# Attention's softmax join and division: from VectorE to GpSimd

## The chip, the cores and the metric

The kernel runs on one core of one Trainium2 chip. The metric is the device time of one execution, in microseconds (us); lower is better. The engines are named as in the profile: PE is TensorE's matmuls and PEld its weight loads, DVE is VectorE, ACT is ScalarE, POOL is GpSimd, SP is SyncE, which issues most of the transfers.

## The reference

One layer of a decoder on 1024 tokens of width 1024 in float32. A normalised input is projected; two token mixers work on the projections; their outputs are gated, merged, projected and added to the input; a gated MLP with a short convolution follows, and a last normalisation. The change is in the two mixers:

```
# differential attention, 4 heads, causal, two softmaxes a head
logits = where(dist >= 0, s - slope * dist, NEG_INF)
p = softmax(logits)
a = p[:, :, 0] - lam * p[:, :, 1]
o = a @ v
o = rmsnorm(o, subln_w) * (1.0 - lam_init)

# sliding-window attention, 8 heads, window 128, one sink logit a head
p = softmax(concatenate([logits, sink], axis=-1))[..., :-1]
o = p @ v
```

## The kernel before

Matmuls run with operands split into a rounded high part and a low part (`wh`, `wl`; `xh`, `xl`), three matmuls for one product. The attention runs as six units in a row: the four heads of the differential attention (`da_step`, `da_av`, `da_norm`), and the two groups of four heads of the windowed attention (`sw_step`). Each unit goes over eight blocks of 128 queries.

A step of the differential attention, `da_step(h, i)`, has width w = (i + 1) * 128, from 128 to 1024 columns. For each of the two softmaxes, c = 0 and 1, TensorE makes the scores into a PSUM tile `sc` (L619); DVE adds the bias, writes the tile `L` and keeps the row's minimum (L623, with a read of its accumulator); ScalarE takes the exponential in place with the row's sum (L624). The first softmax is not divided by its sum: the head's normalisation, `da_norm`, takes that out. So only one factor, -lam * sum0 / sum1, is needed, made by a reciprocal (L627) and a small product (L628), and the join is one DVE instruction (L629). TensorE then turns the joined tile in blocks of 128 x 128 (L635), ScalarE copies the turned blocks out of PSUM as the high part `aT` (L637), DVE subtracts for the low part (L638), and after every second step `da_av` multiplies with the values (L647 to L649).

The L tiles have four buffers (`bufs=4`), so two steps fit in; the aT tiles have five. GpSimd clears the unused half of an aT tile (L602) and takes the power in the head's normalisation (L170).

A step of the windowed attention, `sw_step(g, n)`, holds four heads of up to 256 keys in one L tile: scores (L707), the sink's column copied in by GpSimd (L711), four reductions by DVE (L714), four exponentials (L716), one reciprocal for four sums (L717), a column cleared by GpSimd (L719), four divisions by DVE (L721), transpositions (L728), copies (L731, L732), the product with the values (L738) and the output (L740, L745).

Between these, TensorE works on the projections of the gates, which nothing in the attention needs (`back_half`, matmuls of the tile `g` at L153 to L155). How many halves of them go to each step is written in the table `HALVES`; the scheduler of the framework sets the final order of each engine's instructions by its own estimates, and fixes it when the program is built. Each engine then runs its list in order.

`self.last`, set at the last division, holds back one later product of GpSimd (L776, in `rest`) by an explicit dependency.

Of the kernel before, what the change touches and what calls it, by code (L numbers as in the profile page):

```python
# [13 lines left out]
ALU = mybir.AluOpType  # L14
# [28 lines left out]
class Trunk:  # L43
# [561 lines left out]
    def da_step(self, h, i, st, aT):  # L605
        nc, ap = self.nc, self.ap
        q, k = st
        slope = 4.0 ** -(h + 1)
        w = (i + 1) * P

        lo = P if w == 640 else 0
        cuts = ((0, 256),) if i == 0 else ((0, w),) if w <= H2 else ((0, H2 - lo), (H2 - lo, w))
        pr = []
        for c in range(2):
            sc = self.tl(self.psS, [P, T], "sc")
            qs = q[c][:, i * P:(i + 1) * P]
            for part in range(2):
                for n0, n1 in cuts:
                    nc.tensor.matmul(sc[:, lo + n0:lo + n1], qs, k[c][part][:, n0:n1], start=part == 0, stop=part == 1)  # L619
            L = self.tl(ap, [P, T], "L", bufs=4)  # L620
            s = self.tl(self.st, [P, 4], "sm", bufs=8)
            o = 896 - i * P
            nc.vector.tensor_tensor_reduce(L[:, :w], sc[:, lo:lo + w], self.bias[:, o:o + w], slope, 3e38, ALU.add, ALU.min, s[:, 0:1])  # L623
            nc.scalar.activation(L[:, :w], L[:, :w], AF.Exp, bias=s[:, 0:1], scale=-1.0, accum_out=s[:, 1:2] if c else self.s0[:, i:i + 1])  # L624
            pr.append(L)

        nc.vector.reciprocal(s[:, 2:3], s[:, 1:2])  # L627
        nc.vector.tensor_scalar(s[:, 3:4], self.s0[:, i:i + 1], s[:, 2:3], self.neglam, ALU.mult, ALU.mult)  # L628
        nc.vector.scalar_tensor_tensor(pr[0][:, :w], pr[1][:, :w], s[:, 3:4], pr[0][:, :w], ALU.mult, ALU.add)  # L629
        qo = (i % 2) * P  # L630
        for j0 in range(0, i + 1, 4):
            nj = min(4, i + 1 - j0)
            ps = self.tl(self.psT, [P, 4, P], "t")
            for j in range(nj):
                nc.tensor.transpose(ps[:, j, :], pr[0][:, (j0 + j) * P:(j0 + j + 1) * P], self.ident)  # L635
            hi, lo = aT[j0 // 4, 0], aT[j0 // 4, 1]
            nc.scalar.copy(hi[:, :nj, qo:qo + P], ps[:, :nj, :])  # L637
            nc.vector.tensor_tensor(lo[:, :nj, qo:qo + P], ps[:, :nj, :], hi[:, :nj, qo:qo + P].bitcast(F32), ALU.subtract)  # L638
# [57 lines left out]
    def sw_step(self, g, n, st):  # L696
        nc, ap = self.nc, self.ap
        q, k = st
        k0 = max(n - 1, 0) * P
        w = P if n == 0 else 256  # L700
        bo = T + (P if n == 0 else 0)
        sc = self.tl(self.psS, [P, 4, 256], "sc")
        s = self.tl(self.st, [P, 4, 4], "sw", bufs=4)
        L = self.tl(ap, [P, 4, 256], "L", bufs=4)
        for h in range(4):
            for part in range(2):
                nc.tensor.matmul(sc[:, h, :], q[h][:, n * P:(n + 1) * P], k[part][:, k0:k0 + 256], start=part == 0, stop=part == 1)  # L707


        a, at, we = (0, w, w + 1) if n == 0 else (1, 0, w)  # L710
        nc.gpsimd.tensor_copy(L[:, :, at:at + 1], self.nsink[:, 4 * g:4 * g + 4].unsqueeze(2))  # L711
        for h in range(4):
            slope, ns = 2.0 ** -(4 * g + h + 1), self.nsink[:, 4 * g + h:4 * g + h + 1]
            nc.vector.tensor_tensor_reduce(L[:, h, a:w], sc[:, h, a:w], self.bias[:, bo + a:bo + w], slope, ns, ALU.add, ALU.min, s[:, 0, h:h + 1])  # L714
        for h in range(4):
            nc.scalar.activation(L[:, h, :we], L[:, h, :we], AF.Exp, bias=s[:, 0, h:h + 1], scale=-1.0, accum_out=s[:, 2, h:h + 1])  # L716
        nc.vector.reciprocal(s[:, 3, :], s[:, 2, :])  # L717
        if n:
            nc.gpsimd.memset(L[:, :, 0:1], 0.0)  # L719
        for h in range(4):  # L720
            self.last = nc.vector.tensor_scalar(L[:, h, a:w], L[:, h, a:w], s[:, 3, h:h + 1], None, ALU.mult)  # L721
        po = self.tl(self.psT, [P, H2], "t")
        nblk = w // P
        parts = []
        for b in range(nblk):
            ps = self.tl(self.psT, [P, 4, P], "t")
            for h in range(4):
                nc.tensor.transpose(ps[:, h, :], L[:, h, b * P:(b + 1) * P], self.ident)  # L728
            pt = self.tl(ap, [P, 2, 4, P], "aT", F32R, bufs=5)
            hi, lo = pt[:, 0], pt[:, 1]  # L730
            nc.scalar.copy(hi, ps)  # L731
            nc.vector.tensor_tensor(lo, ps, hi.bitcast(F32), ALU.subtract)  # L732
            parts.append((hi, lo))
        for b, (hi, lo) in enumerate(parts):
            kb = k0 // P + b
            va = self.vsw[kb // 4][:, kb % 4, g]
            for m, pt in enumerate((hi, lo)):
                nc.tensor.matmul(po, va, pt, start=b == 0 and m == 0, stop=b == nblk - 1 and m == 1)  # L738
        t = self.tl(self.gpool, [P, 4, P], "g", bufs=2)[0:64]
        nc.scalar.copy(t, po[64:128].rearrange("p (h q) -> p h q", h=4))  # L740
        pv = po[0:64].rearrange("p (c e q) -> p c e q", c=2, e=2)
        tv = t.rearrange("p (c e) q -> p c e q", e=2)
        y = self.tl(ap, [P, 2, P], "ys", bufs=3)
        for e in range(2):
            nc.vector.tensor_tensor(y[64 * e:64 * e + 64], pv[:, :, e], tv[:, :, e], ALU.add)  # L745
        self.store(self.yd[4 + 2 * g:6 + 2 * g, :, n * P:(n + 1) * P].rearrange("c p q -> p c q"), y)
# [525 lines left out]
```

## Time and profile before

| what | before |
|---|---|
| median of 3 runs | 1345.26 us (1344.66 to 1346.1) |
| span of the profiled execution, first to last instruction | 1343.0 us |
| mean granted TensorE clock | 0.997 |
| differential attention, about | 258 to 398 us |
| windowed attention, about | 398 to 485 us |

The profile shows one execution: its span is 1343.0 us, and a run's time is some 2.3 us above that, as the time includes what lies around the first and the last instruction. Only the span is known of the profiled execution itself. In rows of groups stand the line, the engine, the operation, the tile written and the tiles read, the shape, the count, then the busy time in us, the mean of one in ns, and the idle time just before them with what ended it. A busy TensorE is not a TensorE at its peak: the ends of matmuls are modelled, and a matmul's length overlaps the next one's.

### The profile page before, as it was taken

To read this page: it belongs to the slowest core of one execution; us is meant where nothing else is said; L and a number is where in the kernel's file an instruction comes from. 1 tells how busy PE (TensorE), PEld (TensorE's weight loads), DVE (VectorE), ACT (ScalarE), POOL (GpSimd) and SP (SyncE) were. 2 spreads that over 40 slices of the span, in tenths; PEclk is the share of its full clock that TensorE was granted. 3 is DMA by queue.
4 is the path that set the end of the run, shared out by engine and by line. 5 is a ranking of instruction groups with operands and counts; after the bars stand their busy time and mean duration, and the time that the engine had idled before them with its cause. 6 is when DMAs were issued, how large, how long until landed. Compare 5 with 4: busy or idle time off the path is not lost.

```text
span 1343.0 us, 17167 instructions
## 1 busy us (share of the span) xinstructions
PE 1326.8 (99%) x6304; PEld 1105.7 (82%) x6304; DVE 1052.5 (78%) x1425; ACT 602.3 (45%) x929; POOL 488.8 (36%) x364
## 2 busy tenths in 40 slices
PE   8999999999999999999999999999999999999997
PEld 6888888888888878888888888888888888788886
DVE  7846775388898976445669999999999998967454
ACT  8432232276667774344444434343434345432433
POOL 0346652000101016642446566666666611131011
PEclk9999999999999999999999999999999999999998
DMA  7244443966554245324522222222222239642342
GB/s 258 108 146 162 148 149 119 273 170 189 143 148 144 70 155 206 141 95 130 167 79 95 79 79 85 88 79 79 88 85 80 86 128 320 220 145 98 94 141 79
DMA packets 63812, 179.49 MB, mean 134 GB/s; under 512 B 7024, under 2 KB 16880, under 8 KB 63728
## 3 DMA queue, kind: packets, MB, share of 16 engines
q1 hardware_dynamic: 52272, 161.22, 36.8%
q10 hardware_dynamic: 11456, 17.18, 3.5%
q8 instruction: 50, 0.82, 0.2%
q14 instruction: 34, 0.28, 0.1%
HBM read 129.61 MB, written 48.76 MB: 133 GB/s over the span
## 4 chain that ended last, share of the span: by engine, by line
PE 72%; DVE 15%; issue 8%; DMA 2%; ACT 1%; POOL 1%; SPq 0%; POOLq 0%; DVEq 0%; ACTq 0%
PE t L887 24%; PE g L153 4%; PE g L154 4%; PE g L155 4%; DVE c L1031 3%; PE y L1056 3%; PE d L1056 3%; PE sc L154 3%; PE sc L155 3%; PE sc L153 3%; PE d L887 3%; PE sc L619 3%; PE y L887 2%; DVE wl L113 2%; DMA hr<-hd 2%
## 5 line engine op out<-in xcount | busy, mean ns | idle before, releaser
L1020 POOL TENSOR_TENSOR us<-us,rstd 128x1024 f32<-128x1024 f32 x42 | 92.6, 2225 | 85.0 <-DVE us L452 47.6
L1029 ACT ACTIVATE c<-us,vecs 128x1024 f32<-128x1024 f32 x44 | 54.8, 1248 | 118.3 <-POOL us L1020 113.8
L132 ACT CAST wh<-raw 128x1024 fp32r<-128x1024 f32 (+2 forms) x58 | 58.7, 1012 | 107.9 <-PE sc L154 35.8
L134 DVE TENSOR_TENSOR wl<-raw,wh 128x1024 fp32r<-128x1024 f32 (+2 forms) x58 | 78.3, 1352 | 32.5 <-ACT wh L132 22.8
L113 DVE TENSOR_TENSOR sl<-sf,sh 128x1024 fp32r<-128x1024 f32 x62 | 89.3, 1442 | 12.8 <-ACT sh L111 12.8
L111 ACT CAST sh<-sf 128x1024 fp32r<-128x1024 f32 x62 | 64.5, 1042 | 61.6 <-PE t L887 44.0
L97 POOL TENSOR_TENSOR sf<-rv 128x512 f32<-128x512 f32 x30 | 51.3, 1711 | 93.6 <-DVE sl L113 51.1
L1031 DVE SCALAR_TENSOR_TENSOR c<-us,vecs,c 128x1024 f32<-128x1024 f32 x44 | 75.4, 1746 | 2.7 <-ACT c L1029 2.7
L99 POOL TENSOR_TENSOR sf<-raw,rv 128x512 f32<-128x512 f32 x30 | 56.7, 1891 | 46.3 <-DVE sl L113 46.3
L1032 DVE SCALAR_TENSOR_TENSOR c<-us,vecs,c 128x1024 f32<-128x1024 f32 x44 | 73.2, 1696 | 0.0
L153 PE MATMUL g<-xh,wh 128*128 128x512 f32 x176 | 71.0, 403 | 1.5 <-ACT g L548 1.5
L154 PE MATMUL g<-xl,wh 128*128 128x512 f32 x176 | 70.3, 400 | 0.0
L155 PE MATMUL g<-xh,wl 128*128 128x512 f32 x176 | 70.3, 399 | 0.0
L170 POOL TENSOR_TENSOR rs<-ms,mhalf 128x8 f32<-128x8 f32 (+2 forms) x9 | 13.5, 1499 | 155.5 <-DVE ms L168 149.4
L1012 ACT ACTIVATE c<-c 128x1024 f32<-128x1024 f32 x22 | 23.4, 1064 | 89.6 <-DVE c L1032 89.6
L113 DVE TENSOR_TENSOR wl<-raw,wh 128x1024 fp32r<-128x1024 f32 (+1 forms) x35 | 61.8, 1765 | 0.3 <-ACT wh L111 0.2
L602 POOL MEMSET aT<- 128x128 f32 x32 | 6.1, 204 | 151.5 <-PE t L648 101.2
L623 DVE CUSTOM_DVE_ANT_0 L<-sc,bias 128x128 f32<-128x128 f32 (+7 forms) x64 | 47.8, 752 | 16.6 <-PE sc L619 13.7
L98 POOL TENSOR_TENSOR sf<-sf,raw 128x512 f32<-128x512 f32 x31 | 58.2, 1877 | 2.2
L624 ACT ACTIVATE L<-L,sm 128x128 f32<-128x128 f32 (+7 forms) x64 | 49.6, 778 | 20.0 <-DVE sm L623 17.3
L776 POOL TENSOR_TENSOR gr<-gr,rstd 128x1024 f32<-128x1024 f32 x16 | 40.3, 2523 | 43.9 <-DMA gr<-gd 43.7
L113 DVE TENSOR_TENSOR wl<-rv,wh 128x512 fp32r<-128x512 f32 x30 | 54.0, 1800 | 2.6 <-ACT wh L111 2.6
(435 smaller groups left out, 4338.4 us busy)
## 6 DMA issues: line engine op xcount, KB each, us to landing
u<-qd SPq DMA_DIRECT2D x72, 256.0 KB, 6.4
raw<-in_w_down SPq DMA_DIRECT2D x27, 512.0 KB, 3.7
hr<-hd SPq DMA_DIRECT2D x50, 256.0 KB, 4.8
raw<-in_w_up SPq DMA_DIRECT2D x23, 512.0 KB, 3.5
raw<-in_w_in SPq DMA_DIRECT2D x22, 512.0 KB, 3.8
hd<-c SPq DMA_DIRECT2D x22, 512.0 KB, 2.6
rv<-in_w_up SPq DMA_DIRECT2D x21, 512.0 KB, 3.5
gr<-gd SPq DMA_DIRECT2D x16, 512.0 KB, 3.4
```

The costliest lines, as they stand in the source:

```text
L111: cast = nc.scalar.copy(hi, src)
L113: low = nc.vector.tensor_tensor(lo, src, hi.bitcast(F32), ALU.subtract)
L132: self.hi = nc.scalar.copy(wh, raw)
L134: self.lo = (eng or nc.vector).tensor_tensor(wl, raw, wh.bitcast(F32), ALU.subtract)
L153: nc.tensor.matmul(ps, wh[:, kc + o, :], ah, start=first and n == 0, stop=False)
L154: nc.tensor.matmul(ps, wh[:, kc + o, :], al, start=False, stop=False)
L155: nc.tensor.matmul(ps, wl[:, kc + o, :], ah, start=False, stop=last and n == len(kcs) - 1)
L887: nc.tensor.matmul(ps, (ah, ah, al)[p][:, k, :], (bh, bl, bh)[p], start=first and n == p == 0, stop=last and p == 2 and n == len(ks) - 1, ...
L1020: i = (nc.vector if m % NF == 0 else nc.gpsimd).tensor_tensor(us[:, 2:], us[:, 2:], self.rstd, ALU.mult)
L1031: nc.vector.scalar_tensor_tensor(c, us[:, 1:T + 1], cw[1], c, ALU.mult, ALU.add)
L1032: nc.vector.scalar_tensor_tensor(c, us[:, 0:T], cw[0], c, ALU.mult, ALU.add)
L1056: nc.tensor.matmul(ps, v[:, n, :], x, start=n == i == 0, stop=n == len(js) - 1 and i == 2)
```

## The change

The join of the two softmaxes, one instruction of DVE, becomes two instructions of GpSimd: a product by a scalar per row, in place in the second tile, and an addition into the first. The four divisions of a windowed step go to GpSimd as they are. Lines behind the first edit move down by one.

```diff
         nc.vector.reciprocal(s[:, 2:3], s[:, 1:2])
         nc.vector.tensor_scalar(s[:, 3:4], self.s0[:, i:i + 1], s[:, 2:3], self.neglam, ALU.mult, ALU.mult)
-        nc.vector.scalar_tensor_tensor(pr[0][:, :w], pr[1][:, :w], s[:, 3:4], pr[0][:, :w], ALU.mult, ALU.add)
+        nc.gpsimd.tensor_scalar(pr[1][:, :w], pr[1][:, :w], s[:, 3:4], None, ALU.mult)
+        nc.gpsimd.tensor_tensor(pr[0][:, :w], pr[0][:, :w], pr[1][:, :w], ALU.add)
...
         for h in range(4):
-            self.last = nc.vector.tensor_scalar(L[:, h, a:w], L[:, h, a:w], s[:, 3, h:h + 1], None, ALU.mult)
+            self.last = nc.gpsimd.tensor_scalar(L[:, h, a:w], L[:, h, a:w], s[:, 3, h:h + 1], None, ALU.mult)
```

The framework's scheduler builds a new order from this: in the attention, the instructions of all engines stand in another order than before.

## The prediction

> **What bounds the kernel now.** I read the page first, then a table of the two attention stages by time, then TensorE's matmuls in the second of them.
>
> ```profile
> span 1343.0 us, 17167 instructions
> PE 1326.8 (99%) x6304; PEld 1105.7 (82%) x6304; DVE 1052.5 (78%) x1425; ACT 602.3 (45%) x929; POOL 488.8 (36%) x364
> ```
> ```profile
> 258.00:398.00 140.00, 139.92 (x877) 122.15 (x877) 118.53 (x310) 93.55 (x220) 11.50 (x37) 1.00 0.63 167
> 398.00:458.00 60.00, 59.57 (x367) 51.24 (x366) 54.75 (x191) 45.95 (x131) 5.87 (x22) 1.00 0.38 118
> 458.00:485.00 27.00, 25.40 (x137) 20.30 (x136) 25.07 (x81) 19.49 (x55) 1.67 (x7) 1.00 0.28 86
> ```
>
> Behind the length of each stretch stand the busy times of PE, weight loads, DVE, ACT and POOL, then clock and DMA. TensorE is busy nearly all the time, and the changed lines run only here: differential attention from 258 to 398 us, the windowed attention from 398 to 485. DVE is busy for 85% of the first and 92% of the second ((54.75 + 25.07) of 87), GpSimd for 8 to 9%. So DVE is a near second bound, and GpSimd is idle.
>
> A busy share hides short waits, so I price the matmuls. From the chain of waits, and from the groups of TensorE between 398 and 485 us:
>
> ```profile
> 248.56 0.87 PE t L589 x8
> 1247.69 5.44 PE y L1056 x24
> ```
> ```profile
> L153 PE MATMUL g<-xh,wh 128*128 128x512 f32 x54 | 22.5, 416 | 1.5 <-ACT g L548 1.5
> L154 PE MATMUL g<-xl,wh 128*128 128x512 f32 x54 | 22.0, 408 | 0.0
> L155 PE MATMUL g<-xh,wl 128*128 128x512 f32 x53 | 21.5, 406 | 0.0
> L728 PE MATMUL t<-ident,L 128*128 128x128 f32 x116 | 19.1, 275 | 0.2 <-DVE ys L745 0.2
> L738 PE MATMUL t<-aT,v 128*128 128x512 f32 x56 | 18.7, 404 | 0.4 <-DVE aT L732 0.4
> L707 PE MATMUL sc<-u,u 128*128 128x256 f32 x112 | 18.5, 291 | 0.0
> ```
>
> A matmul of 512 columns advances TensorE by 5.44 / 24 = 0.227 us, one of 256 by half of that, a transposition by 0.87 / 8 = 0.109. The rows make 217 x 0.227 + 112 x 0.113 + 116 x 0.109 = 74.6 us; the other 59 of the 504 matmuls are small and make at most 6.7. So about 81 of 87 us are work, and nearly 6 us are waits and change-overs. The first stretch, counted in the same way, has about 6 of 140. That is the ceiling of any gain: TensorE's work is not changed. As change-overs stay, I put the waits at 2.5 us in the first stage and at 4 us in the second.
>
> **What is removed and added.** DVE's groups in the attention stages, then GpSimd's instructions by line (shortest, median and longest ns):
>
> ```profile
> L629 DVE SCALAR_TENSOR_TENSOR L<-L,sm,L 128x128 f32<-128x128 f32 (+7 forms) x32 | 26.1, 816 | 0.6
> L721 DVE TENSOR_SCALAR L<-L,sw 128x255 f32<-128x255 f32 (+1 forms) x64 | 18.5, 341 | 0.4
> ```
> ```profile
> L776 POOL TENSOR_TENSOR gr<-gr,rstd x16: 2392/2406/3406, 488.1 to 582.3; 128x1024 f32<-128x1024 f32 x16
> L848 POOL TENSOR_TENSOR rstd<-rstd,t x14: 1288/1662/1843, 614.5 to 683.3; 128x512 f32<-128x512 f32 x14
> L602 POOL MEMSET aT<- x32: 204/204/207, 236.4 to 391.5; 128x128 f32 x32
> L1019 POOL MEMSET us<- x44: 89/99/122, 684.8 to 1097.3; 128x2 f32 x44
> ```
>
> DVE loses 26 us of 118 and 18 of 80, some 67 to 78% stay busy. GpSimd gets 32 multiplications, 32 additions and 64 divisions. The addition has two inputs: the first two rows give 0.17 us plus (2.406 - 1.288) / 512 = 2.18 ns a column. The multiplication and the division read one tensor and a scalar per row; before has no such row on GpSimd. From below I bound it by the memsets, which only write: 0.10 us plus (204 - 99) / 126 = 0.83 ns a column. From above stands the two-input rate. I take the memset rate, as a stream with one input is nearer to it, and keep the other end for the range. At width 1024 the multiplication is then 0.95 us (dear: 2.41) and the addition 2.41, at 896 0.84 and 2.12, at 768 0.74 and 1.84, one division of 255 columns 0.31 (dear: 0.73). For a head's eight widths (4608 columns) that makes 16 us of GpSimd in some 34: throughput is enough. What counts is the length of each step's chain: at the mean width of 576 a step has 0.58 + 1.42 = 2.0 us on GpSimd where DVE had 0.82, at 1024 it has 3.4.
>
> The Trainium skill ("GPSIMD Engine Reference", section 4.1) says the same of one-input operations, about line rate, but advises against two-input arithmetic there, as about half as fast as on VectorE. No run so far shows the first. By its figure of one element a cycle at 1.2 GHz, 1024 columns would be an estimated 0.85 us, and the sum would fall by about half a microsecond.
>
> **The first stage.** The chain of a step, from groups by form of 258 to 398 us:
>
> ```profile
> L623 DVE CUSTOM_DVE_ANT_0 L<-sc,bias 128x1024 f32<-128x1024 f32 x8 | 9.7, 1216 | 0.1
> L628 DVE TENSOR_SCALAR sm<-s,sm,neglam 128x1 f32<-128x1 f32 x32 | 8.7, 271 | 0.3
> L623 DVE CUSTOM_DVE_ANT_0 L<-sc,bias 128x768 f32<-128x768 f32 x8 | 7.6, 952 | 0.5 <-PE t L635 0.3
> L638 DVE TENSOR_TENSOR aT<-t,aT 128x512 fp32r<-128x512 f32 x22 | 15.0, 687 | 2.2 <-ACT aT L637 2.1
> L623 DVE DVE_READ_ACCUMULATOR2_ANT sm<- 128x1 f32 x64 | 5.4, 84 | 0.0
> L627 DVE RECIPROCAL sm<-sm 128x1 f32<-128x1 f32 x32 | 5.1, 159 | 1.7 <-ACT L L624 1.7
> ```
> ```profile
> L624 ACT ACTIVATION_READ_ACCUMULATOR L<-L,sm 128x1 f32 x64 | 12.2, 191 | 0.0
> L624 ACT ACTIVATE L<-L,sm 128x1024 f32<-128x1024 f32 x8 | 9.2, 1159 | 0.0
> L624 ACT ACTIVATE L<-L,sm 128x768 f32<-128x768 f32 x8 | 7.5, 936 | 1.0 <-DVE sm L623 1.0
> ```
>
> From the last score matmul to the transpositions, a step of width 768 needs 0.95 + 0.08 + 0.94 + 0.19 + 0.16 + 0.27 = 2.59 us, 0.25 for hand-overs (an allowance of 0.05 each), and 2.58 on GpSimd: 5.4. TensorE can spend that on other matmuls, and the orders of the two built programs tell how many it has. The scheduler has put the transpositions closer to the scores than before: the matmuls between make for step 7 of the four heads 9.3, 8.5, 9.6 and 7.8 us before, and 5.3, 6.9, 7.9 and 6.7 after. The covers shrink while the real chain grows.
>
> New waits come in as well. The four L buffers hold two steps, and the buffer of the second softmax comes free only when GpSimd's addition has read it: 30 of the 64 reductions (L623) in DVE's order now wait for GpSimd, where none did, and DVE's later work queues behind them. GpSimd's own queue has 32 memsets of aT among the new work, which wait for TensorE (that waiting cost nothing while GpSimd was idle).
>
> The tightest places are the ends of the heads. In head 1, step 5's addition ends, DVE reduces step 7's first score (1.30), then has two copies of step 5's aT, which wait for its transpositions and ScalarE, and only about 4.8 us after that addition comes step 7's second reduction (1.30), ahead of the scalar (0.27) that step 6 needs; with 0.84 + 2.12 on GpSimd its sum is ready after 9.4 us. TensorE's order has 5.4 us from step 5's transpositions to step 6's, and step 5's cover of 7.7 less the chain of 5.4 gives 2.2 more: 1.8 us of stall. From step 6 to step 7 GpSimd alone needs 0.95 + 2.41 = 3.4, where the order has 2.2: 1.2 more. Head 2, the same way: 0 and 1.2. Head 3: 0.4 and 3.4 - 1.8 = 1.6. In head 0 step 7's scalar stands behind a reduction of the next head that waits for step 6's addition and another that waits for step 6's transpositions: 0.8 + 0.4 + 0.4 + 3.4 + 0.25 = 5.2 against 3.7 of cover, 1.5 us. Together 7.7 us. Off go the waits of before, 2.5: the stage is 5.2 us longer.
>
> **The second stage.** The divisions lie between the four exponentials and the transpositions. DVE, which was 92% busy, loses 4 x 0.34 = 1.4 us of a step of some 5.4 (87 us for 16 steps).
>
> ```profile
> L731 ACT CAST aT<-t 128x512 fp32r<-128x512 f32 x30 | 17.2, 588 | 8.6 <-PE t L728 6.9 <-DVE sw L714 1.2
> L716 ACT ACTIVATE L<-L,sw 128x256 f32<-128x256 f32 x56 | 28.0, 505 | 1.3 <-DVE sw L714 1.3
> L716 ACT ACTIVATION_READ_ACCUMULATOR L<-L,sw 128x1 f32 x64 | 12.2, 191 | 0.0
> L714 DVE CUSTOM_DVE_ANT_0 L<-sc,bias,nsink 128x255 f32<-128x255 f32 x56 | 24.6, 475 | 0.2 <-PE sc L707 0.2
> ```
>
> Four divisions at 0.31 are 1.25 us, no longer than DVE's 4 x 0.34. The chain is about 0.56 for the first reduction, 4 x 0.70 for the exponentials, 0.5 for reciprocal and hand-overs and 1.25, less the 0.7 by which the reductions start before the last score: 4.4, and up to 1.8 more when three copies out of PSUM at 0.59 stand between them on ScalarE. The covers in the new order are 5.1 to 12.3 (before 7.0 to 16.2); two are under 6.2, for some 2 us of stall. The sink copies and memsets (L711, L719) share GpSimd's queue with the divisions, and a copy that waits for a step's transpositions holds the next step's divisions; that is 1.7 us from transpositions to transpositions, under the 2 us and more that the order has. So -4 + 2 = -2 us.
>
> Downstream the orders of all engines are those of before, but for one gate load on SyncE that goes ahead of four loads. The sum: +5.2 - 2 = +3.2 us, and an allowance of 1.5 for DVE and GpSimd holding each other at the weight splits of these stages (rival 2; 3.44 - 1.21 = 2.2 us each, mostly under the spare time that DVE now has): span 1347.7, and with the 2.3 us that lie around the span (1345.26 less 1343.0) **1350.0 us**.
>
> **Rivals.** (1) GpSimd's one-input rate is that of two inputs. Steps 6 and 7 of each head then pay 1.3 + 1.5 us more, 11 us, and five windowed steps with covers under 7 us pay 1.65 minus what they spare, about 5: 1366 us. For it: nothing on GpSimd here reads one long tensor. Against it: the memsets.
>
> (2) The shared port. In the timeline:
>
> ```profile
> 506.66 6.65 POOL L776 TENSOR_TENSOR gr<-gr,rstd 128x1024 f32<-128x1024 f32 x2 [12.90 <-DMA gr<-gd]
> 507.61 3.44 DVE L134 TENSOR_TENSOR wl<-raw,wh 128x1024 fp32r<-128x1024 f32 x1
> 510.97 1.21 DVE L787 TENSOR_TENSOR gr<-gr,sc 128x1024 f32<-128x1024 f32 x1
> ```
>
> The split L134, with two operands in SBUF, took 3.44 us beside a product of GpSimd; L787, with one operand in PSUM and the same size, 1.21. The Trainium skill ("SBUF — State Buffer", the section on the shared port pair) has it as an exclusive lock, which also a tensor_scalar of VectorE in its two-port mode takes; the rows agree for L134. If the small L628 were held too, a step would lose up to a GpSimd instruction at its scalar; at 0.5 us for half of the steps, 8 us: 1358. Most reductions and copies here read PSUM, which speaks against more.
>
> (3) Faster: the covers have enough play, and what decides is DVE, freed of 44 us. That holds if the additions end within the covers, with under 3 us of stall in all; then the waits of before (2.5 + 4) go for that: 1341.5 us. The 92% of DVE in the second stage speak for it, the shorter covers against it.
>
> (4) It comes out even: stalls at the heads' ends and the gain in the second stage cancel, 1345 us.
>
> **Chances.** Forecast 0.42, rival 1 0.16, rival 2 0.05, rival 3 0.17, rival 4 0.20. With 0.2% (2.7 us, about what a measurement of this kernel can tell from no change) that is slower 0.63, same 0.20, faster 0.17. The range of 1342 to 1366 holds the forecast and its neighbours, and leaves out the further half of rivals 1 and 3. The likeliest case alone spans 1348 to 1355.
>
> **What would show it.** DVE's busy time falls by 44 us; the multiplication at 1024 columns near 0.95 us (2.4 means rival 1); TensorE's idle or stretched time lies before the transpositions (L636 of the changed file) of steps 6 and 7, released by GpSimd; the stretch to 485 us gets shorter in its second part. If transpositions of all steps wait, or L628 grows beyond 0.3 us, rival 2 holds; if none waits for GpSimd, I am wrong about the covers.

## The result and the profile after

The changed kernel takes **1434.0 us** (median of four runs, 1433.35 to 1436.21) where the kernel before takes 1345.1: a ratio of 1.066, 95% interval 1.0648 to 1.0678. It is 6.6% slower. The forecast was 1350.0, the range ended at 1366.

The page of the kernel after, span and busy times:

```profile
span 1431.7 us, 17239 instructions
PE 1353.0 (95%) x6304; PEld 1115.5 (78%) x6304; DVE 1013.9 (71%) x1329; ACT 604.2 (42%) x929; POOL 646.9 (45%) x492
```

VectorE loses 38.6 us of work and GpSimd gains 158. Where the 88.7 us of span went is read from the first and the last transposition of a joined tile (L635 before, L636 after) and the last product with the values of the windowed attention (L738, L739). Each row gives shortest, median and longest ns, then the first and the last start. Of before:

```profile
L635 PE MATMUL t<-ident,L x144: 270/272/332, 267.4 to 397.5; 128*128 128x128 f32 x144
L738 PE MATMUL t<-aT,v x60: 389/395/499, 408.9 to 487.5; 128*128 128x512 f32 x60
```

Of after:

```profile
L636 PE MATMUL t<-ident,L x144: 270/273/477, 269.6 to 453.8; 128*128 128x128 f32 x144
L739 PE MATMUL t<-aT,v x60: 387/393/757, 464.9 to 574.8; 128*128 128x512 f32 x60
```

The first stage ends at 453.8 instead of 397.5: +56.3 us. From there to the last windowed product it is 121.0 instead of 90.0: +31.0. Everything behind that accounts for the last 1.4. Below, "the first stage" of a kernel is always its first to last transposition, 130.1 us before and 184.2 after. In the table by time of the kernel after (PE, weight loads, DVE, ACT, POOL, granted clock), TensorE, which was hardly idle in these stages before, is busy for 149 of 193 us:

```profile
258.00:451.00 193.00, 149.28 (x843) 123.73 (x841) 94.70 (x271) 93.12 (x214) 108.68 (x98) 0.95 0.46 123
451.00:512.00 61.00, 50.93 (x282) 40.70 (x282) 31.33 (x101) 31.89 (x87) 32.07 (x46) 0.97 0.32 99
512.00:575.00 63.00, 54.20 (x272) 42.14 (x271) 36.93 (x116) 36.84 (x103) 36.62 (x51) 0.95 0.21 64
```

GpSimd is not saturated: 109 of 193. So it is no lack of throughput. What an instruction on it costs, by shape, with VectorE's small scalar L628 beside it:

```profile
L722 POOL TENSOR_SCALAR L<-L,sw 128x255 f32<-128x255 f32 x56 | 53.0, 964 | 5.3 <-DVE sw L718 4.9
L629 POOL TENSOR_SCALAR L<-L,sm 128x1024 f32<-128x1024 f32 x4 | 11.4, 2846 | 2.6 <-ACT L L624 2.6
...
L630 POOL TENSOR_TENSOR L<-L,L 128x1024 f32<-128x1024 f32 x4 | 9.4, 2350 | 0.2
...
L628 DVE TENSOR_SCALAR sm<-s,sm,neglam 128x1 f32<-128x1 f32 x32 | 8.7, 272 | 0.7
...
L629 POOL TENSOR_SCALAR L<-L,sm 128x512 f32<-128x512 f32 x4 | 6.3, 1569 | 5.4 <-DVE sm L628 4.8 <-PE t L636 0.6
```

The addition is where the forecast had it (2.35 us, forecast 2.41). The multiplication takes 2.85 us, three times the 0.95 that was taken, and lies above the dear end of 2.41 too: the operation with one tensor costs more than the one with two. A division takes 0.96, not 0.31. The waits of the attention stages (us in total, times, longest):

```profile
DVE L L623 <- POOL L L630: 57.8, 25, 7.0
POOL L L629 <- DVE sm L628: 52.4, 9, 30.8
...
PEld t L636 <- POOL L L630: 44.5, 20, 5.0
ACT L L624 <- DVE sm L623: 43.9, 26, 5.5
PE t L636 <- POOL L L630: 36.4, 20, 4.6
...
PEld t L729 <- POOL L L722: 25.9, 39, 1.0
```

The first line was not in the profile before. VectorE's reductions (L623), the first thing of a step, wait 25 times for GpSimd's addition, and ScalarE and TensorE wait behind them. The timeline of the second head shows the circle (start, length; in brackets the idle time before, with what ended it):

```profile
335.12 1.53 POOL L630 TENSOR_TENSOR L<-L,L 128x640 f32<-128x640 f32 x1
336.68 1.09 DVE L623 CUSTOM_DVE_ANT_0 L<-sc,bias 128x896 f32<-128x896 f32 x1 [3.24 <-POOL L L630]
...
337.70 0.27 DVE L628 TENSOR_SCALAR sm<-s,sm,neglam 128x1 f32<-128x1 f32 x1
...
338.17 2.21 POOL L629 TENSOR_SCALAR L<-L,sm 128x768 f32<-128x768 f32 x1 [1.52 <-ACT aT L638]
...
340.46 1.80 POOL L630 TENSOR_TENSOR L<-L,L 128x768 f32<-128x768 f32 x1
342.29 1.23 DVE L623 CUSTOM_DVE_ANT_0 L<-sc,bias 128x1024 f32<-128x1024 f32 x1 [2.51 <-POOL L L630]
```

The addition of width 640 frees an L buffer; 0.03 us later the reduction of width 896 starts in it. In VectorE's list the factor of width 768 (L628) stands behind that reduction, though it needs nothing of it. Only then can GpSimd multiply for 768, add, and free the buffer for the reduction of width 1024. (The bracket of that multiplication names ScalarE's copy, which ended last; the factor ended at 337.97, 0.2 us before the start, and in the step before, too, GpSimd started 0.2 us after its factor.) VectorE, GpSimd and the buffers form a ring, in which one step's time on GpSimd can't lie beside the next one's.

In the windowed stage the four divisions of a step are a block of 3.7 us in front of its transpositions. Again the timeline:

```profile
491.83 3.67 POOL L722 TENSOR_SCALAR L<-L,sw 128x255 f32<-128x255 f32 x4 [0.68 <-DVE sw L718]
...
495.55 1.05 PE L729 MATMUL t<-ident,L 128*128 128x128 f32 x4 [0.58 <-POOL L L722]
```

### The profile page after: what moved, and what is told of

Read it like the earlier page. It is cut to its first block, busy times and chain, and to the rows that moved or that the text cites. A ratio compares the mean times of both kernels' runs of the same rounds, so it can differ in the third digit from the quotient of the medians.

```text
span 1431.7 us, 17239 instructions
## 1 busy us (share of the span) xinstructions
PE 1353.0 (95%) x6304; PEld 1115.5 (78%) x6304; DVE 1013.9 (71%) x1329; ACT 604.2 (42%) x929; POOL 646.9 (45%) x492
## 4 chain that ended last, share of the span: by engine, by line
PE 81%; POOL 10%; DVE 4%; issue 3%; ACT 2%; DMA 0%; POOLq 0%; ACTq 0%; SPq 0%; DVEq 0%
PE t L888 41%; POOL L L629 4%; PE y L1057 3%; PE d L1057 3%; PE sc L153 3%; PE sc L155 3%; PE sc L154 3%; POOL L L722 3%; PE d L888 3%; POOL L L630 3%; PE g L154 3%; PE g L155 3%; PE g L153 3%; PE y L888 2%; PE d L1084 2%
## 5 line engine op out<-in xcount | busy, mean ns | idle before, releaser
L1030 ACT ACTIVATE c<-us,vecs 128x1024 f32<-128x1024 f32 x44 | 54.8, 1248 | 121.0 <-POOL us L1021 115.5
L623 DVE CUSTOM_DVE_ANT_0 L<-sc,bias 128x128 f32<-128x128 f32 (+7 forms) x64 | 47.8, 753 | 78.6 <-POOL L L630 57.8
L134 DVE TENSOR_TENSOR wl<-raw,wh 128x1024 fp32r<-128x1024 f32 (+2 forms) x58 | 75.2, 1299 | 38.4 <-ACT wh L132 28.7
L629 POOL TENSOR_SCALAR L<-L,sm 128x128 f32<-128x128 f32 (+7 forms) x32 | 56.1, 1752 | 75.4 <-DVE sm L628 52.4
L624 ACT ACTIVATE L<-L,sm 128x128 f32<-128x128 f32 (+7 forms) x64 | 49.7, 778 | 44.7 <-DVE sm L623 43.9
L722 POOL TENSOR_SCALAR L<-L,sw 128x255 f32<-128x255 f32 (+1 forms) x64 | 57.7, 919 | 9.4 <-DVE sw L718 9.0
L619 PE MATMUL sc<-u,u 128*128 128x512 f32 (+2 forms) x192 | 53.7, 382 | 8.5 <-DVE sm L623 7.3
L636 PE MATMUL t<-ident,L 128*128 128x128 f32 x144 | 26.1, 313 | 37.7 <-POOL L L630 36.4
```

The costliest lines, as they stand in the source:

```text
L134: self.lo = (eng or nc.vector).tensor_tensor(wl, raw, wh.bitcast(F32), ALU.subtract)
L629: nc.gpsimd.tensor_scalar(pr[1][:, :w], pr[1][:, :w], s[:, 3:4], None, ALU.mult)
L722: self.last = nc.gpsimd.tensor_scalar(L[:, h, a:w], L[:, h, a:w], s[:, 3, h:h + 1], None, ALU.mult)
```

## The experiments

The leading theory ("A" in the expectations) was that the ring makes the steps run one after the other, so that each microsecond on GpSimd is paid; its rivals were that parts are independent, that a shared resource is held, or that only the longest instructions overfill a step. Kernel before on the same chips: 1344.6 to 1345.2 us.

**The join alone** on GpSimd, divisions back on VectorE:

```diff
-            self.last = nc.gpsimd.tensor_scalar(L[:, h, a:w], ...)
+            self.last = nc.vector.tensor_scalar(L[:, h, a:w], ...)
```

> Only the join of the differential attention is on GpSimd; the windowed divisions are on VectorE as before. In the changed kernel the first stage (258 to 451 us) took 193 us where before took 140, the second (451 to 575) 124 against 87. If the two losses are independent (each stage is held up by its own chain through GpSimd), this gives +53: 1398 us. If the first stage's loss is partly won back later (gate projections that were pushed out of a stage fill the next), it is less, 1380 or so, and the second edit alone costs more than its 36.

1409.4 us (ratio 1.048, 1.0453 to 1.0514), 11 above the 1398 of independent stages. First stage 185.6 us, as in the changed kernel; its windowed stage is 7.8 us longer than before although its divisions are where they were. The built orders tell why: 21 matmuls of the gates stand behind the first stage instead of in it, which is some 5 us of work.

**The divisions alone** on GpSimd, the join on VectorE:

```diff
-        nc.gpsimd.tensor_scalar(pr[1][:, :w], ...)
-        nc.gpsimd.tensor_tensor(pr[0][:, :w], ...)
+        nc.vector.scalar_tensor_tensor(pr[0][:, :w], pr[1][:, :w], s[:, 3:4], pr[0][:, :w], ALU.mult, ALU.add)
```

> Only the windowed divisions are on GpSimd. Independent stages: +36, 1381 us. If GpSimd's throughput bound the stage (4 x 0.93 = 3.7 us a step, 16 steps, 60 us, under the 87 of before) there would be no loss, 1345 us; if a step's divisions, transpositions, copies and the next step's reciprocal follow each other without overlap, a step takes 7.5 us as in the changed kernel, 1381 us.

1358.2 us (1.010, 1.0073 to 1.0132), between the 1345 and the 1381 of the expectation. Waits of its windowed stage:

```profile
PEld t L728 <- POOL L L721: 16.9, 26, 1.0
...
PE t L728 <- POOL L L721: 10.4, 24, 0.6
```

The divisions take 58 us against 18.5 on VectorE; 14.8 of the 39 more are paid, the rest lies beside TensorE's work. Both halves alone add up to 64.8 + 13.6 = 78 of the 89 us. The other 11 go with the order: TensorE's work between a windowed step's last score and its first transposition averages 9.7 us in this kernel's order and 8.2 in the changed one's (11.2 before), counted by the prediction's lengths of a matmul. That link is argued from the orders, not shown by a run.

**The same products at another price**: multiplication and divisions as products of two tensors, the scalar broadcast along the row. The orders of all engines are exactly those of the changed kernel.

```diff
-        nc.gpsimd.tensor_scalar(pr[1][:, :w], pr[1][:, :w], s[:, 3:4], None, ALU.mult)
+        nc.gpsimd.tensor_tensor(pr[1][:, :w], pr[1][:, :w], s[:, 3:4].to_broadcast([P, w]), ALU.mult)
```
(and L722 likewise)

> The changed kernel with both GpSimd products written as a two-input product with the scalar broadcast along the row, in the same order of instructions on every engine. The trace prices the two-input form at 0.17 us + 2.18 ns a column and the product by a scalar at 0.28 + 2.51. Theory A (every nanosecond on GpSimd lies on the path, as steps do not overlap): 4 x (8 x 0.11 + 4608 x 0.33 ns) = 9.6 us and 64 x 0.19 = 12 us fall away: 1412 us. Theory B (GpSimd is 56% busy in these stages and only the order of the other engines delays): no change, 1434 us.

1397.6 us (1.040, 1.0366 to 1.0426), below theory A's 1412, as the product came cheaper than it was priced. By form:

```profile
L722 POOL TENSOR_TENSOR L<-L,sw 128x255 f32<-128x255 f32 x56 | 34.5, 648 | 5.2 <-DVE sw L718 4.7
...
L629 POOL TENSOR_TENSOR L<-L,sm 128x1024 f32<-128x1024 f32 x4 | 7.6, 1894 | 2.0 <-DVE sm L628 2.0
```

The broadcast product is the cheapest of the three, 1.89 us at 1024, which no theory had. With nothing else changed, the multiplications of the first stage lose some 18.5 us, and the stage loses 18.0 (184.2 to 166.2): one for one. The 64 divisions lose 19.3, and the windowed stage 15.5 (121.0 to 105.5). This is the cleanest run for theory A.

**Half of the join**: the multiplication on VectorE and the addition on GpSimd, then the other way round (divisions on VectorE in both).

```diff
-        nc.gpsimd.tensor_scalar(pr[1][:, :w], ..., ALU.mult)
+        nc.vector.tensor_scalar(pr[1][:, :w], ..., ALU.mult)
```
```diff
-        nc.gpsimd.tensor_tensor(pr[0][:, :w], ..., ALU.add)
+        nc.vector.tensor_tensor(pr[0][:, :w], ..., ALU.add)
```

> Of the join only the addition is on GpSimd; the multiplication is a tensor_scalar of VectorE, and the divisions are on VectorE. Theory A (the steps of the first stage run one after the other, so that every microsecond of the join lies on the path): against the kernel with the whole join on GpSimd (1409.4) 8 x 0.28 + 4608 x 2.51 ns = 13.8 us a head go, and some 5.4 us of VectorE come (the windowed division, also a tensor_scalar, took 0.34 us for 255 columns), so 1409.4 - 4 x 8.4 = 1376 us. Rival (the long multiplication alone is what overfills a step; without it a step's chain fits beside TensorE's other matmuls): the stage is back at its old length but for the larger share of VectorE, 1345 to 1355 us.

> The other half: the multiplication on GpSimd, the addition on VectorE, the divisions on VectorE. Theory A: 8 x 0.17 + 4608 x 2.15 ns = 11.3 us a head go, about 5.5 us of VectorE come (1.21 us at 1024 columns), so 1409.4 - 4 x 5.8 = 1386 us, and dearer than the kernel with the addition alone. If what counts is the number of changes between engines and not the time on GpSimd, the two halves cost the same. If the additions of VectorE, which read two tensors in SBUF, are held by GpSimd's multiplications (the lock of rival 2), some of them take over 3 us.

1364.5 (1.014, 1.0124 to 1.0162) and 1381.9 us (1.027, 1.0253 to 1.0291). The second is some 4 us under theory A's 1386; the first is 12 better than A's 1376, and the rival's 1345 to 1355 fails. The two halves do not cost the same, so what counts is time. The additions of the second are never held (longest 1.226 us), but only one of the 32 ran beside an instruction of GpSimd. In the first, VectorE's multiplication of 896 columns is held in each head but the first; two stretches of its timeline, without and with an addition of GpSimd beside it:

```profile
291.44 0.69 DVE L629 TENSOR_SCALAR L<-L,sm 128x896 f32<-128x896 f32 x1
...
363.67 1.83 POOL L630 TENSOR_TENSOR L<-L,L 128x768 f32<-128x768 f32 x1 [3.85 <-DVE sm L627]
363.94 2.04 DVE L629 TENSOR_SCALAR L<-L,sm 128x896 f32<-128x896 f32 x1
```

0.69 us becomes 2.04, ending 0.5 after GpSimd's. The Trainium skill ("SBUF — State Buffer", the section on who interferes with whom) has tensor_scalar among the operations of VectorE that can take the port pair shared with GpSimd; these rows agree, and L628, a single column, was never held.

**The ring's two ties**: both reductions of a step ordered behind the factor of the step before; then five L buffers for four (an `f` buffer goes to make room); then both. Divisions on VectorE, so the join alone (1409.4) is the reference.

```diff
+            with self.tc.issue_after(self.factor.ins) if i else nullcontext():
                 nc.vector.tensor_tensor_reduce(L[:, :w], ...)
```
```diff
-            L = self.tl(ap, [P, T], "L", bufs=4)
+            L = self.tl(ap, [P, T], "L", bufs=5)
```

> As the join alone on GpSimd, but on VectorE both reductions of a step are put behind the small product (L628) that makes the factor of the step before. Theory A (in the built order the factor of a step stands behind the next step's second reduction, which waits for a buffer that the step before frees, so that steps run one after the other, about 6.0 us a step): with the order changed a step's multiplication and addition overlap the next one's reductions and exponentials, the stage goes to GpSimd's own 27 us a head and hand-overs, 35 us a head, and the time to 1350 to 1365 us. Theory C (the loss is the length of GpSimd's instructions whatever the order): no change against the join alone, 1398 us.

> The whole join on GpSimd, the divisions on VectorE, five buffers L in place of four (one f buffer goes for the room), the order of VectorE not forced. With the join alone the time was 1409.4 us, with the order forced 1395.5, with both changes 1386.6. If the two ties give back their parts one by one, the buffer alone is worth some 9 us: 1400. If the buffer helps only once the order is right, 1407 to 1411; if it is the buffer that counts, 1390.

> The whole join on GpSimd, the divisions on VectorE, both reductions of a step behind the factor of the step before, and five buffers L in place of four (one f buffer goes for the room). Theory A (the order and the buffers each tie a step's reductions to the addition of the step before; the order alone gave back 14 us of 64): with both ties loosened GpSimd's 25 us of a head's 34 can lie beside TensorE, 1355 to 1375 us, and the waits of the reductions for GpSimd fall from some 50 us to under 20. Rival (what a step has on GpSimd is too long for TensorE's cover whatever the order): 1390 us or more.

1395.5 (1.038, 1.035 to 1.041), 1393.3 (1.036, 1.0267 to 1.0448) and 1386.6 us (1.031, 1.0289 to 1.0326): 14, 16 and 23 of 64 us come back. The two runs of the buffers alone differ by 5.7 us, so their place between the 1390 and the 1400 of the expectation is not told. The forced order alone did not do what A expected of it. Its timeline shows what took the place:

```profile
332.04 1.56 POOL L631 TENSOR_TENSOR L<-L,L 128x640 f32<-128x640 f32 x1
333.64 0.96 DVE L624 CUSTOM_DVE_ANT_0 L<-sc,bias 128x768 f32<-128x768 f32 x1 [1.27 <-POOL L L631]
...
335.90 0.27 DVE L629 TENSOR_SCALAR sm<-s,sm,neglam 128x1 f32<-128x1 f32 x1
...
336.34 2.21 POOL L630 TENSOR_SCALAR L<-L,sm 128x768 f32<-128x768 f32 x1 [2.74 <-DVE sm L629]
```

The second reduction (here L624) waits for the addition of the step before through the buffer, and GpSimd stands idle for 2.74 us until the factor comes round. With both changes these waits fall from 57 us to 17, as expected, but the time does not fall to 1355 to 1375; TensorE still waits for the additions:

```profile
PEld t L637 <- POOL L L631: 27.6, 13, 3.8
...
DVE L L624 <- POOL L L631: 17.2, 7, 4.8
```

**The join at its cheapest**: order, five buffers and the broadcast product together.

> The join on GpSimd in its cheapest form: forced order, five buffers, and the multiplication as a product of two tensors with the factor broadcast (1.89 us at 1024 columns in place of 2.85); the divisions on VectorE. The kernel with forced order and five buffers took 1386.6 us; the broadcast takes 18.5 us off the join's time on GpSimd. Theory A, one for one: 1368 us. If the clock of TensorE, which fell to 0.94 in that kernel, comes back to 1.00 with the shorter waits, some 8 us more: 1360. If the join fits now beside TensorE's work, 1345 to 1350.

1372.6 us (1.020, 1.016 to 1.0248): 14 of the 18.5 us that the broadcast saves, and still 27 us behind: nearest to theory A's 1368, and far from a join that fits.

**Is it the scalar?** A constant in place of the scalar per row, here and in the divisions:

```diff
-        nc.gpsimd.tensor_scalar(pr[1][:, :w], pr[1][:, :w], s[:, 3:4], None, ALU.mult)
+        nc.gpsimd.tensor_scalar(pr[1][:, :w], pr[1][:, :w], 0.5, None, ALU.mult)
```

> The changed kernel with a constant (0.5) in place of the factor and of the reciprocal sum in GpSimd's multiplications and divisions: it leaves out the true factors, and with them the wait for VectorE's scalar, so its time is not compared; what counts is the length of one multiplication at 1024 columns. If reading a scalar for each row is what made it dear, it falls from 2.85 us to near the 0.95 us of the prediction (or at least under the broadcast form's 1.89); if every one-input product of GpSimd costs this, it stays at 2.8.

By form:

```profile
L629 POOL TENSOR_SCALAR L<-L 128x1024 f32<-128x1024 f32 x4 | 11.1, 2774 | 5.7 <-ACT L L624 5.7
```

2.77 us against 2.85, and 0.86 against 0.96 for a division: reading the scalar costs 0.1 us at most. The price lies in the form of the instruction, one tensor times a scalar. The run, one execution of 1384.7 us, also shows the first stage without the wait for the factor:

```profile
POOL L L629 <- ACT L L624: 39.9, 21, 5.7
```

GpSimd's multiplications now wait for the exponentials, and with 53.3 us of them, where the changed kernel had 56.1, the first stage is 160.0 us, 24 less than there. Its order is its own, and the reductions still wait 24 times for an addition.

**Half of the columns**, the changed kernel first, with its divisions halved in the same way; then the join alone with half of its columns, without and with the ties loosened:

```diff
-        nc.gpsimd.tensor_scalar(pr[1][:, :w], pr[1][:, :w], ...)
-        nc.gpsimd.tensor_tensor(pr[0][:, :w], pr[0][:, :w], pr[1][:, :w], ALU.add)
+        nc.gpsimd.tensor_scalar(pr[1][:, :w // 2], pr[1][:, :w // 2], ...)
+        nc.gpsimd.tensor_tensor(pr[0][:, :w // 2], pr[0][:, :w // 2], pr[1][:, :w // 2], ALU.add)
```

> The changed kernel with GpSimd's three instructions on the first half of their columns only: it leaves out the join and the division of the other half. Theory A (what the join takes beyond VectorE's 26.1 us is paid one for one once some 12 to 22 us of play in the first stage are used up): 4 x (8 x 0.45 + 2304 x 4.66 ns) = 57.3 us in all, 31 more than on VectorE, so 9 to 19 us of stall; 64 divisions of some 0.60 us are 38 us, 20 more than on VectorE, which is within the play of the second stage: 1355 to 1365 us. Rival (what costs is the number of changes between engines and of new waits, which stay the same): over 1400 us.

> The same half-length join with four buffers and the order not forced, the divisions on VectorE. The half-length kernel with the divisions on GpSimd had a first stage 25.9 us longer than before, and its windowed stage 17.8: with the divisions back on VectorE some 1345 + 26 + 5 = 1376 us. Together with the loosened kernel: a difference of 20 us or more is the ties, under 8 us is not.

> Forced order and five buffers L, the join on GpSimd on the first half of its columns only (the join of the other half is left out), the divisions on VectorE. If the ties between steps (a reduction that waits for the addition of an earlier step, and the factor in VectorE's queue behind it) are what the half-length join still pays, 1345 to 1355 us. If a fixed cost of each change to GpSimd is paid whatever the ties, 1365 or more, near the kernel with the same join and the ties left in.

1390.4 (1.034, 1.0292 to 1.0381), 1379.5 (1.026, 1.02 to 1.0318) and 1371.2 us (1.020, 1.0167 to 1.0226). The first missed both expectations: with 57 us of join on GpSimd instead of 101 the stage is 29 us shorter, not 44, and the time neither near 1360 nor over 1400. Its waits say why time on GpSimd is not all:

```profile
POOL L L629 <- DVE sm L628: 79.0, 21, 29.5
DVE L L623 <- POOL L L630: 41.4, 23, 3.1
```

Less the time ahead of the first step (29.5 and 30.8 us, the longest of each), GpSimd waits 49.5 us for the factor where it waited 21.6, and the reductions still wait 23 times for GpSimd where they waited 25 times: shorter instructions leave the ring closed. Loosening it gives 8 us back, just above the 8 that were to speak against the ties, and the two runs with the ties left in differ by 6.6 us. The 1371 us itself lies on the side of the rival (1365 or more). Without the ties loosened, then with them:

```profile
DVE L L623 <- POOL L L630: 42.2, 24, 3.1
```
```profile
PE t L637 <- POOL L L631: 13.4, 13, 1.5
```

With the ties loosened the reductions wait for GpSimd only 4 times, 4.6 us in all, and the first stage falls from 158.3 to 145.0 us. It is still 14.9 longer than before, and TensorE still waits 13 times for an addition. So the ring is not all; whether a fixed cost of each change to GpSimd is in the rest is not shown.

**The prediction's own prices**: the changed kernel with the multiplication on a quarter of its columns, the addition in full and the divisions on 32 columns.

```diff
-        nc.gpsimd.tensor_scalar(pr[1][:, :w], pr[1][:, :w], ...)
+        nc.gpsimd.tensor_scalar(pr[1][:, :w // 4], pr[1][:, :w // 4], ...)
...
-            self.last = nc.gpsimd.tensor_scalar(L[:, h, a:w], L[:, h, a:w], ...)
+            self.last = nc.gpsimd.tensor_scalar(L[:, h, a:w // 8 + a], L[:, h, a:w // 8 + a], ...)
```

> The changed kernel with GpSimd's durations near those of the prediction: the multiplication on a quarter of its columns (0.92 us at width 1024, where 0.95 was assumed), the addition in full, the divisions on 32 columns (some 0.36 us, where 0.31 was assumed); the rest of the products is left out. If the prediction's structure was right and only the price wrong, 1350 us, within 1342 to 1360. If steps run one behind the other through the additions, a step's second-softmax chain sums to 45.1 - 8.8 = 36.3 us a head, 145 for the stage, to which 5 to 18 us came on top in the kernels before: a stage of 150 to 163 where it was 130, 1365 to 1380 us.

1384.7 us (1.030, 1.0246 to 1.0349), above both expectations and far from 1350. The stage is 161.5 us long, within the 150 to 163 of steps in series; the windowed one is 98.0, 8 longer than before. The prices are near the prediction's but not under them: a head's multiplications take 5.4 us for 4.6, a division 0.39 for 0.31. TensorE's transpositions in the first head:

```profile
267.88 0.33 PE L636 MATMUL t<-ident,L 128*128 128x128 f32 x1 [0.58 <-POOL L L630]
270.82 0.44 PE L636 MATMUL t<-ident,L 128*128 128x128 f32 x2 [0.52 <-POOL L L630]
...
298.64 0.69 PE L636 MATMUL t<-ident,L 128*128 128x128 f32 x4 [1.71 <-POOL L L630]
```

All eight steps of this head wait for the addition, 0.5 to 1.7 us each, 8.2 in all.

**One division of four** on GpSimd, join on VectorE, for a kernel that might beat both:

```diff
-            self.last = nc.vector.tensor_scalar(...)
+            self.last = (nc.gpsimd if h == 0 else nc.vector).tensor_scalar(...)
```

> The kernel before with one of the four divisions of a windowed step on GpSimd (the first head's) and three on VectorE. The price of a division on GpSimd is 0.96 us, and it runs beside the three of VectorE (3 x 0.34): if a step pays only what lies on its path, the chain of a step is as long as before, VectorE is 0.34 us shorter in each of 16 steps, and the time is 1340 to 1345 us. Rival (every division on GpSimd costs its time over VectorE's on the path, 13.6 us for four): a quarter of that, 1348 us.

1346.7 us (1.0012, 1.0003 to 1.0021): even this loses 1.6 us, nearer to the rival's 1348 than to the 1340 to 1345. The rows by form, the first of the kernel before:

```profile
L721 DVE TENSOR_SCALAR L<-L,sw 128x255 f32<-128x255 f32 x56 | 16.8, 349 | 0.4
```
```profile
L721 DVE TENSOR_SCALAR L<-L,sw 128x255 f32<-128x255 f32 x42 | 15.6, 415 | 0.3
...
L721 POOL TENSOR_SCALAR L<-L,sw 128x255 f32<-128x255 f32 x14 | 14.2, 1011 | 6.7 <-DVE sw L717 6.3
```

VectorE's own three now take 0.42 us each, where the same shape took 0.35 before; those that run beside a division of GpSimd take up to 0.57. No kernel here beats the one before.

**All stages in one table.** The loop sum is what a step would take if all ran in series from its second reduction to the end of its join, summed over 32 steps. Without the join it is an estimate from rows like those quoted: per head 6.0 (one reduction of each width) + 6.2 (exponentials) + 8 x (0.08 + 0.19 + 0.16 + 0.27) + 8 x 0.25 for hand-overs (an allowance) = 19.8 us. The join adds 25.2 a head in the changed kernel, 6.5 before, and in each other kernel what its own trace shows.

| kernel | time, us | loop sum | first stage, us |
|---|---|---|---|
| before | 1345.1 | 105 | 130.1 |
| changed | 1434.0 | 180 | 184.2 |
| join alone | 1409.4 | 180 | 185.6 |
| broadcast products | 1397.6 | 162 | 166.2 |
| addition on VectorE | 1381.9 | 160 | 165.8 |
| multiplication on VectorE | 1364.5 | 146 | 143.6 |
| the prediction's prices | 1384.7 | 148 | 161.5 |
| half columns / join alone | 1390.4 / 1379.5 | 137 | 155.2 / 158.3 |
| order / buffers / both | 1395.5 / 1393.3 / 1386.6 | 180 | 178.2 / 171.3 / 165.7 |
| both and broadcast | 1372.6 | 162 | 152.4 |
| both and half columns | 1371.2 | 139 | 145.0 |

Where the sum is far above TensorE's 130 us and the ring is closed, the stage is the sum and 4 to 6 us: steps in series. As the sum comes down towards 130, the stage stays 13 to 21 above the sum (the multiplication on VectorE excepted, 2 below it): some steps are then bound by TensorE, others by the ring. With ties loosened it falls 2 to 14 us below the sum (the half columns, near 130, excepted): steps overlap in part. The first stage does not hold the same number of gate matmuls in every kernel: 177 before, 155 in the changed one, 163 with the multiplication on VectorE, 191 with the addition there. At 0.227 us each that is up to 5 us of TensorE's work, so near 130 us differences of that size say nothing.

## Why the prediction was wrong

**The price of the multiplication** is the first step that failed: "I take the memset rate, as a stream with one input is nearer to it". A memset only writes, and nothing in the profile before read and wrote one long tensor. The measured rate is 0.29 us and (2846 - 1569) / 512 = 2.49 ns a column, outside both bounds, since the two-input rate was taken as the dear end. A head's multiplications are 14.0 us, not 4.6, a windowed step's divisions 3.7, not 1.25. The Trainium skill's rule on one-input operations ("GPSIMD Engine Reference", section 4.1), which the prediction could not test, does not hold here: 2.85 us where the estimate by its figure was 0.85. Its advice against two-input arithmetic holds (2.35 us against 1.21 to 1.23 on VectorE).

With prices near the predicted ones the chip gave 1384.7 us. So of the 84 us that the forecast was short, about 49 (1434.0 less 1384.7) are the price and 35 are the structure; the order of that kernel is its own, so the split is good to some microseconds only.

**The stalls "at the ends of the heads"** are the second. The prediction named the parts of the ring: the reductions that wait for additions through the four buffers, and the factor behind the next step's reduction. It then set each step's chain against its own cover, as if a late step left the next one's start alone, and found 7.7 us. Near its own prices the first stage is 31.4 us longer than before, not 5.2, and the first head, put at 1.5 us, waits 8.2 at all eight steps. In the changed kernel the waits are not at the ends of the heads either: all eight steps of the first head wait for their addition, 0.6 to 2.7 us each, and in the other heads steps from the fourth or fifth on. Each step's chain at the measured prices (8.5 us at width 1024), set against its own cover in the changed kernel's order (5.1 to 7.7 at the last steps), gives some 13 us of stall for the stage, which is 54 us longer. What was missing is the carry: in a ring, time that one step overruns its cover is not made up by the cover of the next.

**The windowed stage**, forecast at -2 us, came to +31.0: 5 are matmuls of the gates moved there, the rest goes with the divisions' block of 3.7 us in covers of 8.2 us on average, which is argued and not shown step by step. That VectorE's relief would give 4 us back was wrong in sign even with divisions of 0.39 us (98.0 against 90.0, of which 3 are moved work): the stage was not bound by VectorE's 92%.

**Rival 1**, the one-input rate equal to the two-input one (0.16, 1366 us), had the right mechanism with a price still too low and the same arithmetic of covers. **Rival 2** did not come about: L628 takes 272 ns (271 before), and the weight splits of these stages (L134) average 1.22 us, as long as alone. So the 1.5 us set aside for it were not needed. VectorE can be held, as the run with the multiplication there shows (2.04 us for 0.69), but nothing of the changed kernel's attention was for long. The sign set for this rival, transpositions of all steps that wait, came up in the first head without it. **Rival 3** (1341.5) and **rival 4** (1345) needed the covers. The sign was right, and so were the addition's price and the place where TensorE waits; that VectorE would lose 44 us is 38.6 on the page.

**Open**: what remains with both ties loosened (first stage 165.7 against 130.1), where 7 reductions still wait for an addition; how much is the short cover of the first head and how much the slower clock below was not separated. No run keeps the changed kernel's order with the join on VectorE, so what the new order costs by itself, with its shorter covers, is not shown. More than five L buffers were not tried.

## What to carry to other kernels

Moving work to an idle engine pays only if its time falls off the chain between two waits; an idle engine that takes four times as long makes the chain longer even at 45% load. Before setting a step's chain against its cover, follow the buffers and the queues round once: if an instruction of the next step waits for the moved one, and the moved one's next input stands behind that instruction, the steps are in series, and the sum of the chains, not the largest overrun, sets the time. A price that no row shows is bounded by more than its nearest neighbour; a simple-looking operation can lie outside rows of a plainer and of a richer one.

## What the runs showed of the hardware

On GpSimd in float32, a tensor times a scalar per row costs more (2.85 us at 128 x 1024, 2.77 with a constant) than a sum of two tensors (2.35), and the same product written as two tensors with the second broadcast costs least (1.89).

TensorE's clock followed the stalls. In the kernel with both ties loosened, the timeline has TensorE idle for 2.86 us up to 327.20. By time, with the granted clock in the third column from the end:

```profile
324.00:326.00 2.00, 0.34 (x2) 0.00 (x0) 0.00 (x0) 0.28 (x1) 1.92 (x2) 1.00 0.28 115
326.00:328.00 2.00, 0.80 (x4) 0.73 (x5) 1.68 (x5) 0.82 (x2) 0.28 (x1) 1.00 0.00 0
328.00:330.00 2.00, 2.00 (x11) 1.97 (x10) 0.42 (x2) 0.88 (x4) 0.20 (x1) 0.53 0.00 0
330.00:332.00 2.00, 2.00 (x12) 1.82 (x11) 1.89 (x6) 0.90 (x3) 0.62 (x1) 0.62 0.00 0
332.00:334.00 2.00, 2.00 (x15) 1.73 (x14) 2.00 (x6) 1.03 (x2) 1.92 (x2) 1.00 0.00 0
```

After the idle time comes a stretch of under 4 us at about half speed, then full speed. The Trainium skill ("TensorE: Matmul & The Clock Gate", the section on HAM oscillation) describes this, a fall to half after idle gaps of over about 3.4 us; here a visible gap of 2.9 was enough.

In the changed kernel the granted clock of 0.95 to 0.97 over 317 us is at most 0.05 x 193 + 0.03 x 61 + 0.05 x 63 = 14.6 us of lost matmul time by estimate, part of it in time that the ring would have taken anyway.
